# Block entries with three transposed sums, pooling data in the projection operands' memory, and an earlier begin in the last product

## The chip, the cores and the metric

The kernel runs on one core of one Trainium2 chip, in one launch. Time is device time in microseconds (us), from the start of the program to its end. A core has five engines with queues of their own, which work in parallel and meet through semaphores: TensorE (PE: matmuls and transposes; PEld is its weight load), VectorE (DVE), ScalarE (ACT), GpSimd (POOL) and SyncE (SP), which here only issues DMA transfers. Data lives in DRAM, in SBUF (128 partitions of on-chip memory) and in PSUM (eight banks of 128 x 512 floats, where TensorE writes its results and from which DVE and ACT read).

## The reference

The input is a sequence of 1024 tokens with 1024 channels, in float32. One layer is computed:

```python
h = x + 0.5 * swiglu(rms(x))                    # FFN1: w1, w3 1024 x 2816, w2 2816 x 1024
u = rms(h)
q, k, v, p, gates = split(u @ w_in)             # 3 x 768, 512 and 2 x 1024 columns
yA = dilated_mixture_attention(q, k, v) @ W_A   # 12 heads of 64, 3 groups of dilation 1, 4, 16
yB = multiscale_pool(p) @ W_B                   # 4 groups of 128 channels, windows 2, 4, 8, 16
h = h + (sigmoid(gA) * yA + sigmoid(gB) * yB) @ W_o
h = h + 0.5 * swiglu(rms(h))                    # FFN2
return rms(h)
swiglu(x) = (silu(x @ w1) * (x @ w3)) @ w2
```

`multiscale_pool` takes, for each of its four groups, trailing means over the tokens less the token itself, and applies a 128 x 128 map.

## The kernel before

**Stages.** By the trace, FFN1's up projections run until about 449 us and its down products from there to 670, the projections of the mix stage (`w_in`) from 670 to 1047, attention with the pooling branch and W_o from 1054 to 1302, FFN2 from there to the end. The 1024 tokens are eight tiles of 128 rows; `h[t]` holds tile t.

**Seven products.** Each large matrix product is done by 2 x 2 blocks with seven block products instead of eight. The right-hand blocks of the transposed activations are b11, b12 (tokens 512 to 1023, low channels), b21 (tokens 0 to 511, high channels) and b22. The products use seven sums of them, stored by name in the dictionary X (`SUMS`): b11, b21, b22 and

```python
t1 = b12 - b11;  t2 = b22 - t1;  t4 = t2 - b21;  t3 = b22 - b12
```

Products 1 and 2 use b11 and b21, made from tiles 0 to 3. The products 6, 7, 5, 4 and 3 (in this order) use t2, t3, t1, t4 and b22, which need tiles 4 to 7 as well. `Quad` (L319) does the seven products of one weight block: `operand(m)` makes the weight's sum, `run(m)` multiplies.

**Two parts of each number.** Every operand is held as a rounded part (hi) and a remainder (lo) in TensorE's fast format, and a product is hi·hi + hi·lo + lo·hi: 12 matmuls of 128 x 512 (L314) for one block product. `Sevens.split` makes both parts of a weight: ACT copies the hi part (L303), then POOL or DVE subtracts for the lo part (L306). `Rows` (L372) makes both parts of a token block: four transposes on TensorE into one PSUM bank (L381), ACT's copy of the bank (L382, `x_t`/`x_b` to `xhi`), and, in a later call, DVE's subtraction from the bank (`lower`, L385, `xlo`). PSUM banks come in two sets of four, tagged "mm" and "acc", which are handed out in the order of the program.

**Entries.** There are three places where the sums of a new activation are made: before FFN1's up projections, before the mix projections, before FFN2's up projections (`Entry`, L387; in the rows `f1`, `mix` and `f2`). At first the tiles 0 to 3 are transposed for b11 and b21 (`rows`, `rows_first`, `rows_first2`), beside the last steps of the stage ahead. Then `Entry.run` (L405) walks over the tiles 4 to 7: for each it runs two products i and k that need only b11 or b21 (m of 1 or 2), and between them transposes the tile's five blocks for b22, t1, t2, t4 and t3, 20 transposes in all. t1, t2 and t4 are computed by DVE in SBUF (L423 to L425), t3 by POOL (L426). `high(t, 0)` computes a tile's inverse root mean square (L263 on DVE, L264 on POOL), `high(t, 1)` scales the tile by it and by the gain (L267, 128 x 1024 on DVE); t1 and t3 overwrite the tile of b11 and b21. `operand(i + 2)` and `operand(k + 2)` make the weights of the next two products, `out(i)` takes a product's bank away, `more(n)` makes the weights of the first sum products.

**The order of work.** In all these stages the order of instructions on every engine's queue is that of the program text (`manual_schedule`). An instruction whose data is not there holds everything behind it on its engine.

**Down products.** `Down.run` (L720s) does the product with w2 in seven products m of several steps each. `begin(i)` makes a step's operands: the weights' sum on DVE (L684), hi parts on ACT and lo parts on DVE or, for every fourth, POOL (`bhi`, `blo`, `ahi`, `alo`; L664, L668). `multiply` runs a step's matmuls (L706), `add` adds a finished bank to `h` on DVE (L711), `load(i)` fetches what is needed three steps later. Step i's text is: multiply i, add (of the product before), load i+3, begin i+2. `tick` is a hook used by the first down product alone, where scaling and `rows_first` are hung in.

**End of the mix stage.** The mix loop runs `items` products; jobs near its end load what attention needs: `first_ring` twelve products before the end, values and the first branch weights (`load_values`, `load_branch`, on SP's queue) at the fourth from the end. The pooled groups are stored to DRAM from the mix stage (`pool_dram`, hi and lo). The sums of the mix activations lie in two pools, `xa` (b21, b11) and `xb`, both closed together at the end of the loop.

**Attention.** Its first statements load the four pooled groups, 1 MB each, into four tiles of their own (`load_pool`, L1605, groups 2, 3, 0, 1 in this order), then the queries and keys of the second head group (`load_ring`) and the second branch weights. For each of the 24 block pairs the loop runs scores (L1482), exponents on ACT, transposes, products with the values, and four or eight matmuls of the pooling branch (`branch`, L1619, output `yp`; 12 per product, which reads the four groups in the order 2, 3, 0, 1) as a filler. A finished `yp` is multiplied and stored (`end_branches`, `send`).

Of the kernel before, what the change touches and what calls it, by code (L numbers as in the profile page):

```python
# [16 lines left out]
P = 128  # L17
# [109 lines left out]
def tile_block(  # L127
# [244 lines left out]
    class Rows:  # L372


        def __init__(self, X, what, src, t, tag="acc"):
            q = t % 4
            self.hi, self.lo = (v[:, :, q * P:(q + 1) * P] for v in X[what])
            p = bank(tag, f"x_{what}_{t}")
# [5 lines left out]
        def lower(self):  # L384
            ve.tensor_tensor(self.lo, self.p, self.hi.bitcast(F32), op=OP.subtract)  # L385

    class Entry:  # L387
# [18 lines left out]
        def run(self, high, after, first=0):  # L406
# [3 lines left out]
            y = high(4, 1)  # L410
            for t in range(4, NT):
                i = first + 2 * (t - 4)
                k = i + 1
                self.product(i)
                if t + 1 < NT:
                    high(t + 1, 0)
                lo = self.low[t - 4]
                b11, b21, b12, b22 = lo[:, LOWS], lo[:, HIGHS], y[:, LOWS], y[:, HIGHS]
# [4 lines left out]
                ve.tensor_tensor(t1, b12, b11, op=OP.subtract)  # L423
                ve.tensor_tensor(t2, b22, t1, op=OP.subtract)
# [6 lines left out]
                self.operand(k + 2)  # L431
                rs = [Rows(X, what, src, t) for what, src in (("t1", t1), ("t2", t2), ("t4", t4), ("t3", t3))]
                if t + 1 < NT:
# [191 lines left out]
    class Down:  # L625
# [87 lines left out]
        def run(self, pool, after, tick=None):  # L713
# [6 lines left out]
            for i, (m, s) in enumerate(self.steps):  # L720
# [10 lines left out]
                ahead = i == n - 3 and tick is None  # L731
# [63 lines left out]
    def begin_up1():  # L795
# [23 lines left out]
        def rows(t, what, c):  # L819
            scaled_part(t, c, gain_row)  # L820
            r[t] = Rows(X, what, h[t][:, c], t)
# [27 lines left out]
        rows(3, "b11", LOWS)  # L849
# [5 lines left out]
        entry.operand(1)  # L855

# [16 lines left out]
        r[3].lower()  # L873
        entry.product(3)
# [23 lines left out]
    mstack, dstack = ExitStack(), ExitStack()  # L898
# [5 lines left out]
    def room1():  # L904
        scope.close()
        X_mix.update(sums_of_x(mstack.enter_context(sbuf("xa")), "mix", ("b21", "b11")))
        return down_room("f1")
# [271 lines left out]
    pool_in = {}  # L1179
# [24 lines left out]
    with sbuf("steps1", "right") as pool:  # L1204
# [90 lines left out]
    with tc.manual_schedule():  # L1295
# [4 lines left out]
        for k in range(len(items) + 4):  # L1300
# [27 lines left out]
            if k == len(items) - 12:  # L1328
                later.append([k, first_ring()])
# [823 lines left out]
```

## Time and profile before

| | |
|---|---|
| median of three runs | 1955.8 us (1953.81, 1955.8, 1956.05) |
| the profiled execution | 1956.69 us, its span 1954.5 us |
| mean granted TensorE clock | 0.994 |
| DMA | 333.57 MB, mean 171 GB/s |
| span of FFN1's start and entry, 0 to 66 us | PE busy 61.4 us, DVE 50.8 us |
| FFN1 behind its entry, 66 to 669.7 us | PE busy 602.2 us, DVE 403.5 us |
| mix stage, 669.7 to 1047 us | PE busy 372.1 us, DVE 264.2 us |
| attention to W_o, 1054 to 1302 us | PE busy 235.8 us, DVE 183.0 us, clock 0.96 |
| FFN2, 1302 to the end | PE busy 639.0 us, DVE 439.2 us |

A row of the profile names a line of the kernel (L314 is line 314), an engine, an operation, output and inputs by the program's names (buffer numbers left out), partitions x elements, and how many there are. In the timeline a row begins with its start and its duration, both in us; brackets give the idle time of the engine just before it and what ended it. Times are counted from the span's start. The profiled execution takes 2.2 us more than its span, since a run also holds what lies ahead of the first and behind the last instruction.

### The profile page before, as it was taken

The page shows a single profiled execution, that of the slowest core. Times are in us where ns is not written, and L with a number is a line of the kernel's source. Part 1 is how long each engine was busy: PE and PEld are TensorE (multiplying, and loading weights), DVE is VectorE, ACT ScalarE, POOL GpSimd, SP SyncE. Part 2 cuts the span into 40 slices and gives each one's busy share as a digit, 9 for nine tenths or more (in the row PEclk, how much of TensorE's full clock was granted, in tenths as well). Part 3 has the DMA queues.
Part 4 walks back from the last instruction along what each step waited for, and adds up shares of the span by engine and source line. Part 5 has one row for each costly group of instructions (what it writes and reads, how often), then busy time and mean ns, then how long its engine had stood idle before and what let it go on. Part 6 is the DMA issues. An engine that isn't in the chain of part 4 may idle for free. (4 is left out here: it accounts for less than half of the span.)

```text
span 1954.5 us, 25035 instructions
## 1 busy us (share of the span) xinstructions
PE 1917.3 (98%) x8938; PEld 1580.5 (81%) x8938; DVE 1344.2 (69%) x2020; ACT 762.8 (39%) x1371; POOL 738.1 (38%) x555
## 2 busy tenths in 40 slices
PE   9999999999999999999998999999999999999998
PEld 7788888887888887888876878887788888878886
DVE  7776556557676876658774887787666556577777
ACT  6333333334344533335344663253333333333344
POOL 4433333332223444445454365644333333322131
PEclk9999999999999999999998999999999999999999
DMA  4154223336476437665668887642523222454564
GB/s 185 44 194 164 90 86 113 125 119 214 151 239 213 167 116 235 224 224 183 222 234 281 222 254 253 253 184 78 203 97 128 100 86 103 156 187 138 198 205 162
DMA packets 147437, 333.57 MB, mean 171 GB/s; under 512 B 20208, under 2 KB 40944, under 8 KB 145776
## 3 DMA queue, kind: packets, MB, share of 16 engines
q1 hardware_dynamic: 138096, 307.22, 46.5%
q10 hardware_dynamic: 9216, 24.75, 3.6%
q8 instruction: 71, 1.16, 0.2%
q14 instruction: 54, 0.44, 0.1%
HBM read 229.61 MB, written 102.30 MB: 170 GB/s over the span
## 5 line engine op out<-in xcount | busy, mean ns | idle before, releaser
L706 PE MATMUL d_f<-bhi_f,alo_f 128*128 128x512 f32 x616 | 240.9, 391 | 3.9 <-POOL alo_f L668 3.5
L706 PE MATMUL d_f<-bhi_f,ahi_f 128*128 128x512 f32 x616 | 240.6, 391 | 0.0
L706 PE MATMUL d_f<-blo_f,ahi_f 128*128 128x512 f32 x616 | 239.7, 389 | 0.0
L668 POOL TENSOR_TENSOR alo_f<-g_f,ahi_f 128x512 fp32r<-128x512 f32 x68 | 96.7, 1440 | 287.9 <-ACT ahi_f L664 287.9
L314 PE MATMUL u_mixm<-xhi_t_mix,wc_mixm 128*128 128x512 f32 x608 | 195.8, 392 | 3.3 <-POOL wc_mixm L306 2.4
L314 PE MATMUL u_mixm<-xhi_b_mix,wc_mixm 128*128 128x512 f32 x456 | 149.4, 393 | 1.7 <-DVE y_m L985 1.5
L706 PEld LDWEIGHTS d_f<-bhi_f,alo_f 128*128 128x128 f32 x616 | 115.6, 188 | 31.8 <-POOL alo_f L668 6.5
L314 PEld LDWEIGHTS u_mixm<-xhi_t_mix,wc_mixm 128*128 128x128 f32 x608 | 113.6, 188 | 29.9 <-POOL wc_mixm L306 5.4
L706 PEld LDWEIGHTS d_f<-bhi_f,ahi_f 128*128 128x128 f32 x616 | 115.6, 188 | 24.1 <-ACT ahi_f L664 0.4
L706 PEld LDWEIGHTS d_f<-blo_f,ahi_f 128*128 128x128 f32 x616 | 115.7, 188 | 23.8
L314 PE MATMUL u_mixm<-xlo_t_mix,wc_mixm 128*128 128x512 f32 x304 | 118.5, 390 | 0.0
L306 POOL TENSOR_TENSOR wc_mixm<-s_mixm,wc_mixm 128x512 fp32r<-128x512 f32 x52 | 75.3, 1449 | 99.5 <-ACT wc_mixm L303 77.5
L314 PEld LDWEIGHTS u_mixm<-xhi_b_mix,wc_mixm 128*128 128x128 f32 x456 | 85.5, 188 | 20.7 <-ACT late_hi L1128 1.9
L303 ACT ACTIVATE wc_mixm<-s_mixm 128x512 fp32r<-128x512 f32 x76 | 47.6, 629 | 126.4 <-DVE s_mixm L347 47.9
L314 PE MATMUL u_mixm<-xlo_b_mix,wc_mixm 128*128 128x512 f32 x228 | 88.8, 389 | 0.0
L664 ACT ACTIVATE ahi_f<-g_f 128x1024 fp32r<-128x1024 f32 x84 | 81.8, 974 | 2.7 <-DMA g_f<-gs_f 2.7
L306 POOL TENSOR_TENSOR wc_mixm<-raw,wc_mixm 128x512 fp32r<-128x512 f32 x40 | 59.9, 1502 | 52.6 <-ACT wc_mixm L303 47.6
L664 ACT ACTIVATE bhi_f<-s_f2w 128x512 fp32r<-128x512 f32 x55 | 32.6, 627 | 95.3 <-DVE s_f2w L684 87.6
L1857 PE MATMUL wo<-w_o,o_hi 128*128 128x512 f32 x224 | 69.3, 390 | 0.0
L664 ACT ACTIVATE bhi_f<-s_f1w 128x512 fp32r<-128x512 f32 x55 | 33.0, 630 | 87.0 <-DVE s_f1w L684 82.3
L314 PEld LDWEIGHTS u_mixm<-xlo_t_mix,wc_mixm 128*128 128x128 f32 x304 | 57.1, 188 | 11.9 <-DVE xlo_t_mix L385 0.2
L1619 PE MATMUL yp<-pool_in,wab 128*128 128x512 f32 x192 | 56.4, 431 | 4.8 <-DMA pool_in<-pool 4.8
(1304 smaller groups left out, 5107.1 us busy)
## 6 DMA issues: line engine op xcount, KB each, us to landing
g_f<-gs_f SPq DMA_DIRECT2D x70, 512.0 KB, 4.6
gs_f<-y_f SPq DMA_DIRECT2D x88, 256.0 KB, 2.3
raw<-in_w2a_dram SPq DMA_DIRECT2D x35, 512.0 KB, 4.1
raw<-in_w2b_dram SPq DMA_DIRECT2D x35, 512.0 KB, 4.1
gs_f<-gb_f SPq DMA_DIRECT2D x46, 256.0 KB, 2.3
raw<-in_w1a_dram SPq DMA_DIRECT2D x22, 512.0 KB, 4.6
raw<-in_w3a_dram SPq DMA_DIRECT2D x22, 512.0 KB, 6.3
raw<-in_w1b_dram SPq DMA_DIRECT2D x22, 512.0 KB, 4.6
```

Of the source, the lines that this page charges most:

```text
L303: ac.activation(w[:, 0], src, AF.Copy)
L306: eng.tensor_tensor(w[:, 1], src, w[:, 0].bitcast(F32), op=OP.subtract)
L314: pe.matmul(p, a, b, start=(start and k == 0 and q == 0), stop=(k == 3 and q == 2), skip_group_check=not start)
L664: ac.activation(hi[:, c], src, AF.Copy)
L668: eng.tensor_tensor(lo[:, d], src[:, o], hi[:, d].bitcast(F32), op=OP.subtract)
L706: pe.matmul(self.banks[m][t], l, r, start=(first and q == 0), stop=(last and q == 2))
L1619: pe.matmul(p, a, b, start=(j == 0), stop=(j == 11))
L1857: pe.matmul(banks[m][t], l, r, start=(st == 0 and j == 0 and q == 0), stop=(st == 1 and j == 1 and q == 2))
```

## The change

1. **Entries.** Per tile 4 to 7 only b22, b12 and t3 are transposed: 12 transposes instead of 20. The other sums are built in PSUM by DVE: b12's transposed bank less the kept transposed b11 gives t1, in place; t3's bank plus b11 gives t2, in another bank; t2 less the kept transposed b21 gives t4, in place. The new class `Parts` makes both parts from such a bank, without transposes. The next tile's scaling and its t3 come one tile earlier in the text (`scaled_rows`), and `operand(k + 2)` comes later, behind `fourth()`. The last tile has an order of its own.
2. **Kept blocks.** So that the transposed b11 and b21 are at hand, `Rows.keep` copies the transposed bank back over the half of `h[t]` from which it was made: 8 copies of 128 x 512 on ACT for each of the three entries.
3. **Last product.** In the second down product, in all steps of its last m, `begin(i + 2)` is placed before the adds and the load; before, at one step alone.
4. **Pooling loads.** The four tiles of their own are gone. Groups 2 and 3 are loaded into the two parts of the mix activations' b11 at the fifth product from the end of the mix loop, groups 0 and 1 into b21 at the third from the end, behind the values and the first branch weights. `xa` stays open to the end of attention.

```diff
@@ class Rows
-            p = bank(tag, f"x_{what}_{t}")
+            p = self.flat = bank(tag, f"x_{what}_{t}")
+        def keep(self, dst):
+            ac.activation(dst.rearrange("p (k q) -> p k q", k=4), self.p, AF.Copy)
+
+    class Parts:
+        def __init__(self, X, what, src, t):
+            q = t % 4
+            self.hi, self.lo = (v[:, :, q * P:(q + 1) * P] for v in X[what])
+            self.src = src.rearrange("p (k q) -> p k q", k=4)
+            ac.activation(self.hi, self.src, AF.Copy)
+        def lower(self):
+            ve.tensor_tensor(self.lo, self.src, self.hi.bitcast(F32), op=OP.subtract)
@@ Entry.run
-            y = high(4, 1)
+            def scaled_rows(t):
+                y = high(t, 1)
+                t3 = self.sv.half_tile("s", f"t3_{t}")
+                gp.tensor_tensor(t3, y[:, HIGHS], y[:, LOWS], op=OP.subtract)
+                return y, t3
+            y, t3 = scaled_rows(4)
             for t in range(4, NT):
...
+                last = t == NT - 1
+                b11, b21 = (self.low[t - 4][:, c] for c in (LOWS, HIGHS))
+                def second():
+                    ve.tensor_tensor(t2, r3.flat, b11, op=OP.add)
+                    return Parts(X, "t2", t2, t)
+                def fourth():
+                    ve.tensor_tensor(t2, t2, b21, op=OP.subtract)
+                    return Parts(X, "t4", t2, t)
                 self.product(i)
...
-                s = Rows(X, "b22", b22, t)
-                t1, t3 = b11, b21
-                t2, t4 = (self.sv.half_tile("s", f"{n}_{t}") for n in ("t2", "t4"))
-                ve.tensor_tensor(t1, b12, b11, op=OP.subtract)
-                ve.tensor_tensor(t2, b22, t1, op=OP.subtract)
-                ve.tensor_tensor(t4, t2, b21, op=OP.subtract)
-                gp.tensor_tensor(t3, b22, b12, op=OP.subtract)
-                s.lower()
+                s = Rows(X, "b22", y[:, HIGHS], t)
+                p12 = bank("acc", f"x_b12_{t}")
+                for j in range(4):
+                    c = slice(j * P, (j + 1) * P)
+                    pe.transpose(p12[:, c], y[:, c], ident)
+                r3 = Rows(X, "t3", t3, t)
+                t2 = bank("acc", f"x_t2_{t}")
+                if last:
+                    r2 = second()
+                ve.tensor_tensor(p12, p12, b11, op=OP.subtract)
+                r1 = Parts(X, "t1", p12, t)
+                if not last:
+                    s.lower()
                 self.operand(i + 2)
                 self.out(i)
                 self.product(k)
-                self.operand(k + 2)
-                rs = [Rows(X, what, src, t) for what, src in (("t1", t1), ("t2", t2), ("t4", t4), ("t3", t3))]
-                if t + 1 < NT:
-                    y = high(t + 1, 1)
-                for r in rs:
-                    r.lower()
+                if last:
+                    r2.lower()
+                    r3.lower()
+                    r1.lower()
+                    self.more(1)
+                    r4 = fourth()
+                    s.lower()
+                    r4.lower()
+                else:
+                    y, t3 = scaled_rows(t + 1)
+                    r2 = second()
+                    r1.lower()
+                    r3.lower()
+                    r2.lower()
+                    r4 = fourth()
+                    self.operand(k + 2)
+                    r4.lower()
                 self.out(k)
                 after(t)
-                if t >= NT - 2:
-                    self.more(t - NT + 2)
+                if t == NT - 2:
+                    self.more(0)
@@ Down.run
-                ahead = i == n - 3 and tick is None
+                ahead = tick is None and m == len(DOWN) - 1 and i + 2 < n
@@ FFN1, tiles 0 to 3
-        rows(3, "b11", LOWS)
+        rows(3, "b11", LOWS, "mm")
...
         entry.product(0)
         entry.operand(1)
+        for t in range(4):
+            r[t].keep(h[t][:, LOWS])
...
         squares(5, square2)
         r[3].lower()
+        for t in range(4):
+            r[t].keep(h[t][:, HIGHS])
@@ pooling loads
+    def load_pool(g, x, part):
+        y_pool[g] = X_mix[x][part].rearrange("p (q k) c -> p q (k c)", q=2)
+        nc.sync.dma_start(y_pool[g].bitcast(F32), pool_dram[g])
@@ rows_first of the mix entry, lower(t, rs) of FFN2's
+            for r, c in zip(rs, (LOWS, HIGHS)):
+                r.keep(h[t][:, c])
@@ mix loop
+            if k == len(items) - 5:
+                load_pool(2, "b11", 0)
+                load_pool(3, "b11", 1)
             if k == len(items) - 4:
                 load_values(0, row_part)
                 load_branch(0)
+            if k == len(items) - 3:
+                load_pool(0, "b21", 0)
+                load_pool(1, "b21", 1)
@@ attention
-        for g in (2, 3, 0, 1):
-            load_pool(g)
         load_ring(uses[1], ring_tile)
```

More of the change, by code (lines that the diff above doesn't have):

```diff
@@ L905, in room1 @@
         scope.close()
-        X_mix.update(sums_of_x(mstack.enter_context(sbuf("xa")), "mix", ("b21", "b11")))
+        X_mix.update(sums_of_x(xstack.enter_context(sbuf("xa")), "mix", ("b21", "b11")))
         return down_room("f1")
@@ L1339, in tile_block @@
     left_b = ExitStack()
-    y_pool = [left_b.enter_context(sbuf(f"pool{g}")).tile([P, 2, S], F32R, name=f"pool_in{g}") for g in range(4)]
     sums_o = left_b.enter_context(sbuf("sums_o"))
@@ L1788, in tile_block @@
     left_b.close()
+    xstack.close()
     x2, m1 = ExitStack(), ExitStack()
@@ L1881, in scaled2, with lower @@
         scaled(t, h[t] if t < 4 else rows_y[t], gain2)
-    def lower(rs):
+    def lower(t, rs):
         for r in rs:
             r.lower()
+        for r, c in zip(rs, (LOWS, HIGHS)):
+            r.keep(h[t][:, c])
     with tc.manual_schedule():
```

22 lines of the change are left out of this document (9 added, 13 removed).

## The prediction

> **What bounds the kernel now.** I read the page's busy times first, then TensorE's waits and busy time by stage, then the timeline of the stages that the change touches.
>
> ```profile
> PE 1917.3 (98%) x8938; PEld 1580.5 (81%) x8938; DVE 1344.2 (69%) x2020; ACT 762.8 (39%) x1371; POOL 738.1 (38%) x555
> ```
> ```profile
> 30.00:66.00 36.00, 34.70 (x189) 28.15 (x188) 30.92 (x42) 20.57 (x39) 21.74 (x16) 1.00 0.14 45
> 660.00:704.00 44.00, 43.07 (x228) 35.67 (x227) 34.93 (x50) 24.46 (x46) 25.07 (x19) 1.00 0.19 71
> ...
> 1283.00:1338.00 55.00, 52.51 (x274) 43.08 (x274) 46.15 (x70) 28.11 (x51) 24.94 (x18) 1.00 0.28 100
> ```
> ```profile
> 1050.00:1075.00 25.00, 18.53 (x86) 12.73 (x84) 6.77 (x25) 7.87 (x22) 4.09 (x4) 0.74 1.01 373
> ```
> In a window row the first number is its length, then each engine's busy time, the granted TensorE clock, DMA share and GB/s. TensorE (PE) is busy 98% of the span, so only two things help: fewer matmul slots, or the 37 us in which it is idle or slowed. The three entries (first three rows) hold 1.3, 0.9 and 2.5 us of idle time; the start of attention alone holds 6.5 us, at a mean clock of 0.74. DVE is busy for 31 of 36 us in the first entry: it is the next engine there.
>
> **Part 1, pooling data loaded earlier.** Before, the four loads (L1605, 1 MB each) follow everything else on SP's queue.
>
> ```profile
> PE yp L1619 <- DMA pool_in<-pool: 4.8, 2, 3.5
> ```
> ```profile
> DMA to landing us min/median/max: 9.3/14.0/18.2
> ```
> ```profile
> 1041.24 0.39 PE L314 MATMUL u_mixm<-xhi_b_mix,wc_mixm 128*128 128x512 f32 x1
> ...
> 1054.19 4.40 SPq L1605 DMA_DIRECT2D pool_in<-pool  x4
> ...
> 1064.26 1.63 PE L1619 MATMUL yp<-pool_in,wab 128*128 128x512 f32 x3
> ...
> 1072.33 1.22 PE L1619 MATMUL yp<-pool_in,wab 128*128 128x512 f32 x2 [3.48 <-DMA pool_in<-pool]
> 1073.48 0.58 PE L1482 MATMUL s<-qk_hi,qk_hi 64*128 64x256 f32 x2
> ...
> 1078.21 1.15 ACT L1155 ACTIVATE qk_hi<-qk_in 128x512 fp32r<-128x512 f32 x2 [0.55 <-DMA qk_in<-rot]
> ...
> 1085.52 0.40 PE L1482 MATMUL s<-qk_in,qk_hi 64*128 64x128 f32 x2
> ```
> ```profile
> 1041.40:1047.00 5.60, 5.60 (x27) 4.63 (x26) 1.20 (x2) 5.06 (x10) 5.11 (x5) 1.00 0.24 94
> 1059.00:1077.00 18.00, 11.69 (x53) 7.86 (x53) 5.46 (x28) 7.20 (x21) 0.00 (x0) 0.58 0.99 362
> 1061.80:1065.20 3.40, 2.63 (x8) 1.80 (x9) 0.53 (x3) 2.88 (x12) 0.00 (x0) 0.50 0.99 399
> ...
> 1078.80:1082.20 3.40, 3.40 (x30) 2.93 (x30) 1.90 (x6) 2.53 (x10) 2.55 (x2) 0.99 0.97 333
> ```
> The first pooling product starts at 1064.26; its seventh and eighth matmul, on the third load, wait until 1072.33, and the next scores start at 1073.48. The DMA engines are full all that time (0.99 from 1059 to 1077).
>
> In the changed kernel loads 2 and 3 go into b11's two halves. b11's last reader, the product of the last projection's first sum, ends at about 1041.5 (first timeline row), SP has nothing to issue there before the late weights' store, and from 1041.4 to 1047 the DMA engines are 0.24 busy. 2.1 MB at the 0.42 MB per us of the full stretches is 5.0 us: it fits. Loads 0 and 1 go into b21 behind the values and the first branch weights, so they take the places in the queue that 2 and 3 had: issue at 1054.19, first landing 9.3 us later at 1063.5, before the product starts. Nothing is queued behind a new wait on SP except stores whose data come later anyway.
>
> So the eight matmuls run on: 8 x 0.43 us (half clock, 1.63 us for three overlapping) from 1064.26 is 1067.7, and the scores start 5.8 us earlier. What is late next is the second head group's queries and keys, queued behind the pooling loads: ACT waits for them at 1078.21. They move by the 2.1 MB that left the full stretch, 5.0 us, to 1073.2, and through ACT, the exponents and the key half the scores of that group move from 1085.5 to 1079.5 or 1080.5. I take **5.5 us**; bounds 3 (another queue entry, such as the next branch weights, is the limit) and 8 (the clock returns earlier as well).
>
> The clock is 0.50 in the third row and full again by the fourth; it fell when TensorE had been idle for about 1.3 us waiting for the first exponents, before any pooling wait, so I leave the first fall in and let the second half of the slow stretch go only as far as the loads allow. The Trainium skill, "TensorE: Matmul & The Clock Gate" (Part 1), has the clock halved only after an idle window of about 3.4 us and full after one busy window. The trace disagrees with its first half (an idle stretch much shorter came before the fall). By that rule the changed kernel would keep the full clock there; see the fourth rival.
>
> **Part 2, the entries.** Per tile 4 to 7, five blocks were transposed (20 transposes); now three (12), the other sums being built by DVE in PSUM.
>
> ```profile
> 669.75:677.47 7.72, 7.72 (x45) 6.59 (x44) 6.16 (x9) 5.70 (x11) 4.79 (x4) 1.00 0.11 45
> ```
> ```profile
> 672.96 0.60 PE L381 MATMUL x_t<-ident,h 128*128 128x128 f32 x4
> ...
> 674.62 0.47 PE L314 MATMUL u_mixm<-xhi_b_mix,wc_mixm 128*128 128x512 f32 x1
> ...
> 698.33 0.47 PE L314 MATMUL u_mixm<-xhi_t_mix,wc_mixm 128*128 128x512 f32 x1
> ...
> 702.67 0.73 PE L314 MATMUL u_mixm<-xhi_t_mix,wc_mixm 128*128 128x512 f32 x2 [0.61 <-POOL wc_mixm L306]
> ```
> ```profile
> 676.68 0.68 DVE L423 TENSOR_TENSOR h<-hn_mix,h 128x512 f32<-128x512 f32 x1
> 677.40 0.69 DVE L424 TENSOR_TENSOR s_mixt<-hn_mix,h 128x512 f32<-128x512 f32 x1
> ...
> 679.35 1.93 DVE L267 SCALAR_TENSOR_TENSOR hn_mix<-h,nst,gain_mix 128x1024 f32<-128x1024 f32 x1
> 681.95 2.48 DVE L385 TENSOR_TENSOR xlo_t_mix<-x_t,xhi_t_mix 128x512 fp32r<-128x512 f32 x4 [0.67 <-ACT xhi_t_mix L382]
> ...
> 710.30 0.93 DVE L306 TENSOR_TENSOR wc_mixm<-s_mixm,wc_mixm 128x512 fp32r<-128x512 f32 x1 [0.78 <-ACT wc_mixm L303]
> ```
> ```profile
> 680.15 3.51 POOL L306 TENSOR_TENSOR wc_mixm<-raw,wc_mixm 128x512 fp32r<-128x512 f32 x2
> ...
> 705.69 1.29 POOL L306 TENSOR_TENSOR wc_mixm<-s_mixm,wc_mixm 128x512 fp32r<-128x512 f32 x1 [1.37 <-ACT wc_mixm L303]
> ```
> Removed: 16 transposes took 674.62 - 672.96 = 1.66 us, so one is 0.104 us, 8 are 0.83 us a tile, 3.3 us an entry, 10.0 us in all, if TensorE stays the limit. A tile took 7.72 us with TensorE always busy, and would take 6.89.
>
> But DVE's work per tile does not shrink, and it now has a chain. In order: t1 0.72 (a result used by the next, 676.68 to 677.40), b22's lower half 0.62 (2.48 / 4), the next tile's scaling 1.93, t2 0.62, three lower halves 1.86, t4 0.62, then a wait for ACT's copy of t4, 0.78 (as before L306 at 710.30), its lower half 0.62, the inverse 0.06: 7.8 us from one t1 to the next. No row shows DVE writing a bank; its rows reading one (0.62) and those with both inputs in SBUF beside a busy POOL (1.7) bound it, and I take 0.62 as nearest. Bounds for the tile: 7.2 (scaling at 1.28, as in the clear) and 9.0 (two waits, scaling 2.34).
>
> Behind that chain stands the weight of the next tile's second product (the operand call moved behind t4): t4 ends 6.4 us after t1 starts, ACT's copies of t4 and of the weight take 0.6 each and POOL 1.29 to 1.75, so it is ready at 9.0. Counted from tile 4's first transpose: t1 0.85, tile 5's transposes 6.89 (second product 9.85, late by 1.7), tile 6's 15.35, tile 7's 23.15, last product until 28.2; t2's lower half is ready at 27.4, so the first sum product starts at 28.2 and the next, waiting for its weight as before, at 31.3. Before: 698.33 and 702.4, from 669.75, are 28.6 and 32.6. **Gain 1.3 us**, not 3.3.
>
> ```profile
> 26.03 1.68 POOL L306 TENSOR_TENSOR wc_f10a<-raw,wc_f10a 128x512 fp32r<-128x512 f32 x1 [1.82 <-PE u_f11a L314]
> ...
> 31.30 0.60 PE L381 MATMUL x_b<-ident,x 128*128 128x128 f32 x4
> ...
> 65.10 0.74 PE L314 MATMUL u_f10a<-xhi_t_f,wc_f10a 128*128 128x512 f32 x2 [0.62 <-POOL wc_f10a L306]
> ```
> ```profile
> 681.32 2.07 ACT L382 ACTIVATE xhi_t_mix<-x_t 128x512 fp32r<-128x512 f32 x4 [1.09 <-PE x_t L381]
> ```
> ```profile
> 1302.37 0.60 PE L381 MATMUL x_b<-ident,hn_f 128*128 128x128 f32 x4
> ...
> 1336.37 0.73 PE L314 MATMUL u_f20a<-xhi_t_f,wc_f20a 128*128 128x512 f32 x2 [0.62 <-POOL wc_f20a L306]
> ```
> FFN1's entry has in addition a multiply of 0.6 us on DVE in two tiles, which makes 32.4 to the same point, against 33.5 before (65.10 less 0.3, from 31.30): 1.1 us. But eight copies on ACT are added (0.52 us each by the four in 2.07). The first four fill a pause; the second four stand before ACT's copy of the first m=2 weight, which POOL finishes at 27.7 for a product that starts at 28.5 (2.75 us before 31.30). 2.0 us later there is 1.2 us of stall, 1.0 with POOL in the clear. **Gain 0** (bounds -2.5 and +4). FFN2: 31.9 against 33.7, less 0.5 for copies that hold banks a little longer in front of the transposes of rows 2 and 3: **1.3** (-1.5 to +5). In the mix stage the copies lie beside the down steps and cost nothing; if that cover were gone, 8 x 0.52 = 4.2 us. The memory place of rows 3 in FFN1 (another bank) costs nothing: it only keeps the copies from being waited for.
>
> **Part 3, the last product.**
>
> ```profile
> PE d_f L706 <- POOL alo_f L668: 2.0, 3, 0.8
> ```
> ```profile
> 1934.05 0.50 PE L706 MATMUL d_f<-bhi_f,alo_f 128*128 128x512 f32 x1 [0.74 <-POOL alo_f L668]
> ```
> Operands of the last four steps are now begun before the adds. DVE works without a pause there, the same operations in another order, so the last operand is ready when it was; the 0.74 us at 1934.05 goes, and may come back at the last step. **0.5 us** (-0.5 to 2.0).
>
> **Sum.** 5.5 + 1.3 + 0 + 1.3 + 0.5 = 8.6 us. The profiled execution took 1956.7, so 1948.1; the median of the runs shown is 1955.8, 0.9 under it: **1947.2 us**. Its own range, from the middle of each bound, is 1943 to 1951.
>
> **Rivals.**
> A. TensorE stays the limit in the entries: the 10.0 us of transposes come off whole, and about 2 of the stalls. 5.5 + 12 + 0.5 = 18: 1937.8. For it: DVE was busy only 6.16 of 7.72 us in the first tile. Against: the sum of 7.8.
> B. The wait only moves: attention is held by the next transfers (3.0), the entries break even or lose a little (-1 together): 2 us, 1953.8, no change.
> C. Slower: the weight behind t4 sets the period of each entry tile. From a chain of over 8.3 us a tile loses more than its transposes gave; at the upper bound, 9.0 + 0.7 of POOL contention, 2.0 us over 7.72 in 12 tiles is 24 less the 6 gained elsewhere: 18 us, 1974; at 9.0 alone it is 15 - 6 = 9, 1965. For it: POOL's 3.51 for two, the fixed order of each queue. Against: operands in PSUM keep t1, t2 and t4 clear of POOL.
> D. The clock does not fall at the start of attention: the eight matmuls and the scores after them save 8 x 0.2 + 0.7 = 2.3 us if the keys are there: 1944.9. Against: the exponents' wait stays.
>
> **How the numbers follow.** Forecast 0.50, A 0.12, B 0.20, C 0.10, D 0.08. No change here means within 0.2%, 3.9 us, which is about what a measurement of this kernel can tell. The forecast, A, D and 0.06 of B's 0.20 (its upper bounds) are faster: 0.76; the rest of B is no change, 0.14; C is slower, 0.10. The range 1938 to 1957 holds the forecast, D, B and half of A, and leaves out C.
>
> **What would show it.** Right: the loads of pooling data in two pairs, no yp wait for them, next scores 5 to 6 us earlier after the mix stage; 96 transposes fewer; in the entries TensorE waiting for POOL's weight or a lower half about 1.7 us a tile, DVE without pauses. Wrong: entry tiles at 6.9 us without waits (A), at 9 or more (C), the second group's keys landing no earlier than 1078 (B), a clock of 1.00 at the first pooling product (D).

## The result, and the profile after

| | median (us) | ratio to the kernel before, 95% interval |
|---|---|---|
| before | 1954.29 | |
| changed kernel | 1952.69 | 0.9995 [0.9987, 1.0002] |

The change makes no difference that can be told from none: 1.6 us, where 8.6 were forecast. The profiled execution of the changed kernel took 1955.09 us, its span is 1953.3 us, 1.2 under that of before. Two large parts cancel. First the page's busy times, then the start times of a few tiles' matmuls in both kernels (count, shortest/median/longest in ns, first and last start):

```profile
PE 1910.2 (98%) x8842; PEld 1571.7 (80%) x8842; DVE 1337.3 (68%) x2020; ACT 776.9 (40%) x1395; POOL 725.2 (37%) x555
```
Before:
```profile
L314 PE MATMUL u_f11a<-xhi_t_f,wc_f11a x32: 388/389/389, 89.3 to 100.0; 128*128 128x512 f32 x32
L1619 PE MATMUL yp<-pool_in,wab x192: 387/395/796, 1064.3 to 1195.5; 128*128 128x512 f32 x192
L1857 PE MATMUL wo<-w_o,o_hi x224: 387/389/477, 1203.9 to 1299.2; 128*128 128x512 f32 x112
L314 PE MATMUL u_f28a<-xhi_t_f,wc_f28a x32: 389/389/389, 1620.9 to 1634.3; 128*128 128x512 f32 x32
```
After:
```profile
L314 PE MATMUL u_f11a<-xhi_t_f,wc_f11a x32: 388/389/389, 90.9 to 101.5; 128*128 128x512 f32 x32
L1678 PE MATMUL yp<-xhi_b_mix,wab x96: 387/397/775, 1068.2 to 1191.3; 128*128 128x512 f32 x96
L1915 PE MATMUL wo<-w_o,o_hi x224: 387/389/477, 1200.5 to 1296.4; 128*128 128x512 f32 x112
L314 PE MATMUL u_f28a<-xhi_t_f,wc_f28a x32: 389/389/389, 1619.9 to 1633.3; 128*128 128x512 f32 x32
```

The 96 transposes are gone (8938 - 8842). Read downwards, the changed kernel's lag is +1.6 us behind FFN1's entry (90.9 - 89.3), +3.9 at the first pooling product (1068.2 - 1064.3), -3.4 when W_o starts (1200.5 - 1203.9), -1.0 in FFN2 (1619.9 - 1620.9) and -1.2 at the end. So **attention won 7.3 us** (from +3.9 to -3.4), and what surrounds it gave back 6.1, nearly all of it in the three entries and the copies just ahead of them.

**Attention.** Windows of 3.4 us and the timeline of the changed kernel:

```profile
1063.20:1066.60 3.40, 2.05 (x18) 1.48 (x18) 2.44 (x16) 2.50 (x5) 0.00 (x0) 0.84 1.05 417
1066.60:1070.00 3.40, 3.38 (x10) 2.32 (x11) 1.12 (x2) 2.89 (x12) 0.00 (x0) 0.50 1.00 406
1070.00:1073.40 3.40, 3.40 (x21) 2.40 (x20) 0.66 (x3) 1.12 (x6) 0.00 (x0) 0.65 1.00 402
1073.40:1076.80 3.40, 3.40 (x24) 3.05 (x22) 2.69 (x9) 2.57 (x6) 0.77 (x1) 1.00 0.64 192
```
```profile
1068.17 1.63 PE L1678 MATMUL yp<-xhi_b_mix,wab 128*128 128x512 f32 x3
...
1071.86 0.58 PE L1544 MATMUL s<-qk_hi,qk_hi 64*128 64x256 f32 x2
...
1075.32 1.15 ACT L1206 ACTIVATE qk_hi<-qk_in 128x512 fp32r<-128x512 f32 x2 [0.54 <-DMA qk_in<-rot]
...
1081.67 0.40 PE L1544 MATMUL s<-qk_in,qk_hi 64*128 64x128 f32 x2
```

The eight pooling matmuls run on without a wait. Counted from the first of them, the next scores come 3.69 us later, against 9.22 before (1073.48 - 1064.26): 5.5 us won, where 5.8 were worked out. The second group's keys follow 7.15 us later against 13.95, 6.8 won where 5.0 were worked out, and that group's scores 13.5 against 21.3 (1085.52 - 1064.26), 7.8 won. The clock is full again in the fourth row; by the first three rows it stood at half for about 6.9 us (2 x 3.4 x (0.16 + 0.50 + 0.35)), against 17 before.

**Entries.** TensorE's waits in the changed kernel (sum, times, longest); then the timeline at the end of FFN1's entry, filtered to PE, DVE, ACT and POOL, and the window behind it:

```profile
PE u_f20a L314 <- DVE xlo_t_f L385: 3.2, 1, 3.2
PE u_f10a L314 <- DVE xlo_t_f L385: 3.2, 1, 3.2
PE u_mixm L314 <- DVE xlo_t_mix L385: 3.2, 1, 3.2
...
PE d_f L753 <- ACT ahi_f L711: 1.6, 1, 1.6
PE x_b L381 <- ACT h_again L389: 1.4, 1, 1.4
```
```profile
31.12 0.60 PE L381 MATMUL x_b<-ident,x 128*128 128x128 f32 x4
...
55.03 0.60 PE L381 MATMUL x_t<-ident,s_f1t 128*128 128x128 f32 x4
...
61.95 0.69 PE L314 MATMUL u_f10a<-xhi_t_f,wc_f10a 128*128 128x512 f32 x1 [3.19 <-DVE xlo_t_f L385]
```
```profile
54.91 1.78 DVE L345 TENSOR_TENSOR s_f10a<-raw 128x512 f32<-128x512 f32 x1
56.73 0.69 DVE L347 TENSOR_TENSOR s_f10a<-s_f10a,raw 128x512 f32<-128x512 f32 x1
59.15 0.70 DVE L441 TENSOR_TENSOR x_t<-x_t,x 128x512 f32<-128x512 f32 x1 [1.73 <-ACT xhi_t_f L382]
...
60.51 0.69 DVE L401 TENSOR_TENSOR xlo_t_f<-x_t,xhi_t_f 128x512 fp32r<-128x512 f32 x1
61.12 0.68 DVE L385 TENSOR_TENSOR xlo_t_f<-x_t,xhi_t_f 128x512 fp32r<-128x512 f32 x1
```
```profile
57.51 0.63 ACT L303 ACTIVATE wc_f10a<-s_f10a 128x512 fp32r<-128x512 f32 x1 [2.23 <-DVE s_f10a L347]
58.05 0.58 ACT L382 ACTIVATE xhi_b_f<-x_b 128x512 fp32r<-128x512 f32 x1
58.53 0.59 ACT L382 ACTIVATE xhi_t_f<-x_t 128x512 fp32r<-128x512 f32 x1
```
```profile
54.87 1.28 POOL L306 TENSOR_TENSOR wc_f12b<-raw,wc_f12b 128x512 fp32r<-128x512 f32 x1 [1.95 <-ACT wc_f12b L303]
```
```profile
61.00:64.40 3.40, 2.45 (x6) 2.00 (x7) 3.33 (x7) 1.88 (x5) 0.60 (x1) 0.65 0.00 0
```

The lines are the changed kernel's: L441 makes t2, L460 t1, L445 t4, and L401 is the lower part of `Parts`. Tile 7's three blocks are transposed by 55.6 (last transposes at 55.03). Their copies on ACT (L382) start at 58.05, since ACT's queue has the weight of the first sum product in front (L303 at 57.51, from `more(0)`), and that waits for its sum on DVE (L345 and L347, until 57.4). L345 takes 1.78 us: it reads two tiles in SBUF, while POOL subtracts a weight (L306 at 54.87). t2 (L441) starts 0.03 us after ACT's copy of t3's bank has ended, in all three entries, though both only read that bank; whether the program's bookkeeping or the chip asks for this order was not settled. TensorE's next product needs t2's lower part (L401) and, as will be shown, the bank that t3's lower part (L385) gives back. It stands still for 3.19 us, and then the clock is down to a mean of 0.65 over 3.4 us.

From tile 4's first transpose to the first sum product it takes:

| us | FFN1 | mix | FFN2 |
|---|---|---|---|
| before | 28.87 | 28.58 | 29.07 |
| changed kernel | 30.83 | 30.72 | 31.03 |
| early k+2 alone | 29.01 | 28.74 | 29.94 |
| late weight | 29.02 | 28.90 | 30.66 |
| late weight, early k+2 | 27.24 | 26.96 | 29.58 |
| the same, weight on POOL | 27.25 | 26.98 | 28.13 |
| the same, i+2 and out(k) early | 26.92 | 26.95 | 27.58 |

The last five rows are experiments, told now.

### The profile page after: what moved, and what is told of

It is laid out like the page before. It is cut to its first block, busy times and chain, and to the rows that moved or that the text cites. A ratio compares the mean times of both kernels' runs of the same rounds, so it can differ in the third digit from the quotient of the medians.

```text
span 1953.3 us, 24868 instructions
## 1 busy us (share of the span) xinstructions
PE 1910.2 (98%) x8842; PEld 1571.7 (80%) x8842; DVE 1337.3 (68%) x2020; ACT 776.9 (40%) x1395; POOL 725.2 (37%) x555
## 5 line engine op out<-in xcount | busy, mean ns | idle before, releaser
L306 POOL TENSOR_TENSOR wc_mixm<-s_mixm,wc_mixm 128x512 fp32r<-128x512 f32 x52 | 74.8, 1439 | 101.6 <-ACT wc_mixm L303 84.3
L303 ACT ACTIVATE wc_mixm<-s_mixm 128x512 fp32r<-128x512 f32 x76 | 47.7, 629 | 126.3 <-DVE s_mixm L347 44.4
L306 POOL TENSOR_TENSOR wc_mixm<-raw,wc_mixm 128x512 fp32r<-128x512 f32 x40 | 57.6, 1442 | 66.2 <-ACT wc_mixm L303 62.2
L715 DVE TENSOR_TENSOR alo_f<-g_f,ahi_f 128x1024 fp32r<-128x1024 f32 (+1 forms) x44 | 52.7, 1197 | 7.1 <-ACT ahi_f L711 7.1
```

Source lines behind the costliest of these rows:

```text
L303: ac.activation(w[:, 0], src, AF.Copy)
L306: eng.tensor_tensor(w[:, 1], src, w[:, 0].bitcast(F32), op=OP.subtract)
L715: eng.tensor_tensor(lo[:, d], src[:, o], hi[:, d].bitcast(F32), op=OP.subtract)
```

## The experiments

Times are medians; the kernel before was measured beside each group, at 1953.9, 1953.1, 1952.8 and 1954.3 us. Differences between runs of different groups carry this spread of 1.5 us.

**1. The pooling loads alone, and all but them.** The first is the kernel before with part 4 of the change; the second the changed kernel with the loads back at the start of attention.

```diff
 # first: the kernel before
+            if k == len(items) - 5:
+                load_pool(2, "b11", 0)
+                load_pool(3, "b11", 1)
...
-        for g in (2, 3, 0, 1):
-            load_pool(g)
 # second: the changed kernel, the same lines the other way
```

> The kernel before with the pooling loads alone (part 4 of the change). Theory: the traces of before and after lag by +3.9 us when the first pooling product starts and by -3.4 us when W_o starts, so the loads are worth 7.3 us wherever the rest stands: 7 us under before (5.5 to 8.5). Rival: part of those 7.3 us is only the entries' lag taken up by a wait that was there anyway; then 3 to 4 us under before.

> The changed kernel with the pooling loads where they were. Theory: what is left is the three entries' loss, 1.6 + 2.1 + 1.7 us, less 0.3 at the last product: 5 us over before (3.5 to 6.5), with a wait of about 3.2 us of TensorE before the first sum product in each entry and the half clock behind it. Rival (the loss of the entries is absorbed by the wait for the pooling loads): within 1.5 us of before.

Measured: the loads alone 1947.27 us, ratio 0.9963 [0.995, 0.9977], 6.6 us under before; all but the loads 1957.17, ratio 1.0015 [1.0007, 1.0024], 3.3 us over. The first is as the theory had it; the second shows the loss of the entries by itself, just under the theory's span and far from the rival's absorption. The two parts are separate and of opposite sign. Their sum, 3.3 under before, is 1.7 us more than the 1.6 of the whole change; that rest was not followed up.

**2. The weight of the first sum product later.** `more(0)` is taken from the end of tile 6 and put behind tile 7's transposes, in one kernel ahead of t2, in the other behind t1.

```diff
-                if t == NT - 2:
-                    self.more(0)
...
                 if last:
+                    self.more(0)          # "late weight"
                     r2 = second()
                 ve.tensor_tensor(p12, p12, b11, op=OP.subtract)
                 r1 = Parts(X, "t1", p12, t)
+                if last:
+                    self.more(0)          # the other kernel: here instead
```

> The changed kernel with the weight of the first sum product (more(0)) moved behind the three transposed blocks of tile 7, ahead of t2. Order on DVE is unchanged; on ACT the copies of b22 and t3 now stand ahead of the weight's copy. Theory (ACT's queue): t2 no longer waits for a copy held behind the weight; in FFN1 and mix it starts at the end of the weight's second sum, 1.7 us earlier, the wait of 3.2 us falls to 0.6 to 1.5 and the half clock behind it goes; in FFN2 the lower part of that weight is on DVE ahead of t2 and little is won (0.3): 5 to 9 us under the changed kernel. Rival (DVE's sums are late by themselves, 1.8 us beside POOL, and ACT's order is no matter): within 1 us of the changed kernel.

> As before, but the weight is moved behind t2 and t1 on DVE too. Theory: in FFN1 and mix t2's lower part is ready when TensorE is, the weight's lower part 1.5 to 2.1 us later, so a wait of 1 to 2 us stands at the first sum product's third matmul, and FFN2 wins the same now: 5 to 11 us under the changed kernel, more than the other placement if FFN2 decides. Rival (the weight is the late operand in any order): 0 to 2 us under the changed kernel, waits of 3 us at the weight instead of the lower part.

Measured: ahead of t2 1945.73 us, ratio 0.9953 [0.9941, 0.9966], 7.0 under the changed kernel; behind t1 1947.6, ratio 0.9969 [0.9958, 0.998], 5.1 under. The first kernel's timeline in FFN1's last tile, on ACT, DVE and PE, and the windows behind the first sum product in FFN1, mix and FFN2:

```profile
55.86 0.61 ACT L382 ACTIVATE xhi_t_f<-x_t 128x512 fp32r<-128x512 f32 x1
57.73 0.63 ACT L303 ACTIVATE wc_f10a<-s_f10a 128x512 fp32r<-128x512 f32 x1 [1.27 <-DVE s_f10a L347]
```
```profile
55.13 1.78 DVE L345 TENSOR_TENSOR s_f10a<-raw 128x512 f32<-128x512 f32 x1
...
57.56 0.69 DVE L441 TENSOR_TENSOR x_t<-x_t,x 128x512 f32<-128x512 f32 x1
```
```profile
60.35 0.47 PE L314 MATMUL u_f10a<-xhi_t_f,wc_f10a 128*128 128x512 f32 x1 [1.37 <-DVE xlo_t_f L385]
```
```profile
60.00:63.60 3.60, 3.25 (x14) 2.60 (x15) 3.52 (x6) 2.10 (x4) 1.29 (x1) 1.00 0.00 0
697.00:700.60 3.60, 2.85 (x13) 2.40 (x14) 3.52 (x7) 2.07 (x5) 1.11 (x2) 1.00 0.00 0
1322.40:1326.00 3.60, 3.01 (x8) 2.41 (x9) 3.04 (x6) 2.08 (x5) 1.16 (x1) 0.53 0.01 2
```

The copy of t3 runs 2.7 us earlier, t2 follows the sums at once, TensorE's wait is 1.37 us instead of 3.19 in FFN1 and in mix, and the clock stays at 1.00 behind it. In FFN2, where the weight's lower part stood on DVE ahead of t2, the wait is still 2.8 us and the clock falls to 0.53. The theory holds in all three entries; the rival (ACT's order is no matter) falls. The other placement is not better: its first sum product still waits 1.5 us in FFN1 and mix (by the profile for one of ACT's copies, not for a lower part) and 2.9 in FFN2, so the advantage expected there did not come.

**3. operand(k+2) early, the weight on POOL, and two more places.**

```diff
 # on top of "late weight"
                 else:
+                    self.operand(k + 2)
                     y, t3 = scaled_rows(t + 1)
...
                     r4 = fourth()
-                    self.operand(k + 2)
                     r4.lower()
 # on top of that
-                     lambda n: first.A.operand((6, 7)[n]))
+                     lambda n: first.A.operand((6, 7)[n], (gp, None)[n]))
 # on top of that
                 r3 = Rows(X, "t3", t3, t)
+                self.operand(i + 2)
...
                     r4 = fourth()
+                    self.out(k)
                     r4.lower()
```

> The late weight (more(0) behind tile 7's transposes), and operand(k+2) back in front of the next tile's scaling, as before the change, so that it no longer stands behind t4. Theory (POOL beside DVE): that weight's lower part then runs about 2 us earlier, the first sum of the first sum product (1.78 us beside POOL) takes 0.7 instead, t2 follows 1.1 us earlier, TensorE's wait before the first sum product falls from 1.4 to about 0.3 in FFN1 and mix and from 2.8 to 1.7 in FFN2, whose half clock goes: 3 to 6 us under the late weight alone (1945.7). Rival (the early weight collides with the scaling instead, 1.9 for 1.3, and the tiles get longer): 0 to 3 us over it.

> The same, with the lower part of the first sum product's weight on POOL in FFN1 and FFN2 (only FFN2 changes, there it was on DVE). Theory: DVE is freed of 0.7 us and of a wait of 0.8 ahead of t2, FFN2's wait falls by 1.4: 1 to 2 us under the one with operand(k+2) early. Rival (POOL is later than DVE with it): no change, with a wait for POOL's weight at the third matmul.

> The same as the last, and in each tile operand(i+2) ahead of t1 and out(k) between t4 and its lower part. Theory (ACT's order delays the weight by the copy of t1, DVE waits 0.67 us for ACT's copy of t4): the waits of 0.4 to 0.7 for POOL's weight go, and the tiles come down to 7.2 to 7.5 us: 2 to 5 us under the last. Rival (TensorE is already the limit of the tiles by then): within 1 us of it.

Measured: 1940.64 us, ratio 0.9937 [0.9925, 0.995], 5.1 under the late weight; 1937.39, ratio 0.992 [0.9907, 0.9934], 3.2 under that; 1936.75, ratio 0.9915 [0.9902, 0.9929], 0.6 under that. The first step gave the time that was expected, and FFN2's half clock went, though the waits only fell to 0.70 us in FFN1 and mix and 2.1 in FFN2 (0.3 and 1.7 expected). In the second, FFN2's wait fell from 2.1 to 0.7 us as expected; the rest of its 3.2 us is not in the entries: the two profiled executions, 6.4 us apart, differ by 4 us before FFN2's entry already, with waits for exponents of 3.8 and 1.6 us in attention. The edit does not touch attention, so I take this for spread from one execution to another; that was not shown. The third missed: the tiles were at 7.25 to 7.55 us in FFN1 already, and came to 7.27 to 7.36 only.

**4. operand(k+2) early, alone.** The same move in the changed kernel, with `more(0)` left at the end of tile 6.

> The changed kernel with operand(k+2) back in front of the next tile's scaling, and nothing else. Theory: the first sum of tile 7 runs in 0.7 us beside an idle POOL instead of 1.78, so everything behind it on DVE and ACT comes 1.1 us earlier; the wait falls from 3.2 to 2.1 us in each entry, and at 2.1 the clock stays: 3 us an entry, 6 to 10 us under the changed kernel (1952.7). Rival (only ACT's order counts; POOL's work goes on elsewhere): within 1 us of it.

Measured: 1946.98 us, ratio 0.9964 [0.9951, 0.9976], 5.7 under the changed kernel, a little short of the expected 6. Its timeline on POOL, DVE and PE in FFN1, and the window behind the first sum product:

```profile
51.01 1.29 POOL L306 TENSOR_TENSOR wc_f12b<-raw,wc_f12b 128x512 fp32r<-128x512 f32 x1
```
```profile
54.30 0.68 DVE L345 TENSOR_TENSOR s_f10a<-raw 128x512 f32<-128x512 f32 x1
...
57.43 0.70 DVE L441 TENSOR_TENSOR x_t<-x_t,x 128x512 f32<-128x512 f32 x1 [1.73 <-ACT xhi_t_f L382]
```
```profile
60.23 0.51 PE L314 MATMUL u_f10a<-xhi_t_f,wc_f10a 128*128 128x512 f32 x1 [2.49 <-DVE xlo_t_f L385]
```
```profile
60.00:63.60 3.60, 3.37 (x9) 2.68 (x10) 3.52 (x6) 2.15 (x4) 1.28 (x1) 0.57 0.00 0
```

POOL's subtraction is done before DVE's sum, which takes 0.68 us instead of 1.78, and t2 starts 1.72 us earlier (57.43 against 59.15). But it still waits 1.73 us for ACT's copy of t3, behind the weight. The wait fell to 2.49 us only, since TensorE too came earlier, and the clock still fell (0.57). That part of the expectation was wrong.

**5. The standing time filled.** 24, then 11 matmuls of 128 x 128 without a use behind the last product of each entry, in the changed kernel.

```diff
                 if last:
+                    idle = bank("mm", f"idle_{self.sv.name}")
+                    for _ in range(24):       # 11 in the second
+                        pe.matmul(idle[:, :P], ones, ones, start=True, stop=True)
                     r2.lower()
```

> The changed kernel with 24 matmuls of 128 x 128 without a use put in the wait before the first sum product of each entry (about 2.6 of the 3.2 us). The wait for t2's lower part stays where it is. Theory (the clock falls because TensorE stands still for some 3 us): the clock stays at 1.00 in the rows behind the wait, and each entry ends 1.7 to 2.0 us earlier: 5 to 6 us under the changed kernel (1952.7). Rival (the slow first matmuls have another cause, such as the operands just written): within 1 us of the changed kernel.

> The changed kernel with 11 matmuls of 128 x 128 without a use in the wait before the first sum product, in place of 24: each of the 24 ran as two passes of 0.115 us, and they overran the wait by 2.1 us. 11 are 2.5 us of the 3.2. Theory (the clock falls because TensorE stands still): the clock stays at 1.00 behind the wait, the first sum product starts where it did, and each entry ends 1.7 to 2.0 us earlier: 5 us under the changed kernel (1952.7; 3 to 7). Rival (the clock falls for the data wait, not for the standing): within 1 us of the changed kernel, matmuls 0.43 us apart behind the wait.

Measured: with 24, 1957.31 us, ratio 1.0021 [1.0012, 1.0029], 4.6 over the changed kernel; with 11, 1950.08, ratio 0.9984 [0.9975, 0.9993], 2.6 under. Each matmul ran as two passes, so 24 filled 5.5 us, and the first sum product came 1.9 us late in each entry (in FFN1 32.77 us behind tile 4's first transpose, against 30.83). That is 0.3 us an entry more than the half clock it saves, 1.0 in all; the rest of the 4.6 is open. With 11 they fit. Below: their row, the product behind them and the window; then the first sum product's rows in the changed kernel and in this one.

```profile
59.37 2.62 PE L470 MATMUL idle_f<-ones 128*128 128x128 f32 x22
62.71 0.47 PE L314 MATMUL u_f10a<-xhi_t_f,wc_f10a 128*128 128x512 f32 x1 [0.73 <-DVE xlo_t_f L385]
```
```profile
61.20:64.60 3.40, 2.67 (x15) 2.20 (x15) 3.33 (x7) 1.87 (x5) 0.04 (x1) 1.00 0.00 0
```
```profile
L314 PE MATMUL u_f10a<-xhi_t_f,wc_f10a x32: 389/389/687, 61.9 to 74.3; 128*128 128x512 f32 x32
```
```profile
L314 PE MATMUL u_f10a<-xhi_t_f,wc_f10a x32: 388/389/468, 62.7 to 73.5; 128*128 128x512 f32 x32
```

The wait for data ends where it did (30.85 us behind tile 4's first transpose, against 30.83), but the clock is 1.00 in the windows behind it in all three entries, and this block's products take 10.8 us (62.7 to 73.5) instead of 12.4 (61.9 to 74.3): the half clock costs 1.6 us an entry where it comes. It falls because TensorE stands still: behind the unfilled stands of 2.5 to 3.2 us it fell in ten of eleven places in the profiles of this case, behind the filled ones in none of six. The gain of 2.6 us is just under the expected 3 to 7; three times 1.6 would be 4.8. Part of the rest is lost at once: the next weight block's first sum product (`u_f10b`, `u_f20b`) comes 1.2 us earlier in FFN1 and 1.5 in FFN2 (44.90 and 44.82 us behind tile 4's first transpose, against 46.13 and 46.33). And the falls do not come in every execution. In the changed kernel without the loads, the same program up to the end of FFN1, the profile has the same wait of 3.18 us in FFN1, but the clock stays at 1.00 behind it and the block takes 10.8 us:

```profile
L314 PE MATMUL u_f10a<-xhi_t_f,wc_f10a x32: 388/389/467, 62.3 to 73.1; 128*128 128x512 f32 x32
```

Over the executions of the changed kernel the mean clock ran from 0.992 to 0.997, and the profiled one had 0.993. How often the falls come in the others was not measured.

**6. The last product's order alone,** in the fastest kernel.

```diff
-                ahead = tick is None and m == len(DOWN) - 1 and i + 2 < n
+                ahead = i == n - 3 and tick is None
```

> The fastest version so far (late weight, early operand(k+2), weight on POOL, operand(i+2) early, out(k) early; 1936.75) with the last product's begin order of the kernel before. It measures part 3 alone. Theory (the waits of 2.0 us between the steps go, a wait of 1.4 for the last step's left operand and a half clock come in their place): 0 to 1.5 us over it. Rival (they go for good): 2 us over it.

Measured: 1937.96 us, ratio 0.9918 [0.9904, 0.9931], 1.2 over, as the theory had it; the intervals overlap, so the size is uncertain. In the last 40 to 20 us of the span TensorE is busy 10.00 of 10.00 us in both windows of 10 us of the changed kernel, against 8.70 and 9.26 before; the wait of 1.6 us for the last left operand (`ahi_f` in the waits above) is new. In the changed kernel's profile the clock falls behind this wait too: it is 0.61 from 1940.1 to 1943.5 us, with matmuls 0.43 us apart, and of the change of order only 0.2 us is left (the lead is 1.0 us in FFN2 and 1.2 at the end). It stays at 1.00 there in the profiles of the kernel before and of the fastest kernel.

**7. Which lower part releases the first sum product.** On top of the fastest kernel:

```diff
                     r2 = second()
+                    r3.lower()
+                    r2.lower()
                 ve.tensor_tensor(p12, p12, b11, op=OP.subtract)
...
                 if last:
-                    r2.lower()
-                    r3.lower()
                     r1.lower()
```

> The fastest version so far (1936.75, where TensorE still stands 0.7 us before the first sum product of each entry) with t3's lower part, and behind it t2's, directly behind t2 in tile 7, ahead of t1. Theory (the bank): the first sum product takes over the bank of t3's transposed block, and what releases it in the rows is t3's lower part (L385), 0.15 us before it starts, not t2's (L401), which is ready 0.6 us earlier. With both one place earlier the wait of 0.7 goes in each entry: 1.5 to 2.1 us under. Rival (t2's own lower part, or the weight's on POOL, is what it waits for): the wait stays at 0.5 to 0.7, within 0.6 us of it.

Measured: 1939.08 us, ratio 0.9928 [0.9914, 0.9942], 2.3 over the fastest kernel. TensorE's timeline in FFN1, in the fastest kernel and in this one:

```profile
58.17 0.47 PE L314 MATMUL u_f10a<-xhi_t_f,wc_f10a 128*128 128x512 f32 x1 [0.70 <-DVE xlo_t_f L385]
```
```profile
57.28 0.39 PE L314 MATMUL u_f10a<-xhi_t_f,wc_f10a 128*128 128x512 f32 x1
...
60.73 0.50 PE L314 MATMUL u_f10a<-xhi_t_f,wc_f10a 128*128 128x512 f32 x1 [0.51 <-ACT wc_f10a L303]
...
62.15 0.73 PE L314 MATMUL u_f10a<-xhi_t_f,wc_f10a 128*128 128x512 f32 x2 [0.69 <-POOL wc_f10a L306]
```

The wait of 0.70 us before the first sum product is gone in all three entries. Both lower parts had been moved, so the run alone does not tell them apart, but the rows do: the product starts at 57.28, while t2's lower part (L401) runs until 57.39, and in the changed kernel that part was ready at 61.20, 0.75 us before the product started. So it was t3's lower part, and as the product does not read t3, the bank. But t1 now comes 1.3 us later on DVE and the next weight's sum 0.7, and the second sum product waits 0.51 + 0.69 us for that weight instead: by the next weight block the entry is 0.8 us longer in FFN1 and 0.7 in FFN2 than in the fastest kernel. The mechanism was right, and more than the gain went into the next wait.

## Why the prediction was right in its wide range and wrong in its sum

- **Pooling loads: mechanism right, size low.** 5.5 us were forecast, 7.3 (in the profiles) and 6.6 (alone) measured, inside the bounds of 3 to 8. What was too small is the second group's keys (5.0 worked out, 6.8 measured) and the earlier return of the clock, which only the upper bound named; how the rest splits between them was not shown. The fourth rival (the clock does not fall) did not come: the first fall, at the wait for exponents, stayed (0.84 and 0.50 in the first two windows).
- **The tiles of the entries: right.** In mix, tiles 5, 6 and 7 were to start 6.89, 15.35 and 23.15 us behind tile 4; they started 7.16, 15.35 and 22.89 behind (at 678.76, 686.95 and 694.49, from 671.60). TensorE waited for POOL's weight in them, as forecast, but by 0.2 to 0.7 us where it stands in the rows, not 1.7; and POOL's neighbourhood made DVE no slower where it reads a bank. So the slower rival, a weight that sets the period, did not come, nor did TensorE as the limit.
- **The end of the entries: wrong, and this is the step that failed.** "t2's lower half is ready at 27.4, so the first sum product starts at 28.2": it started at 30.7 in mix and 30.8 and 31.0 in the others. The chain was carried on from tile to tile as if tile 7 were like the rest. Ahead of tile 7 the queues also hold `more(0)`: two sums on DVE, one of them at 1.78 us beside POOL, and a copy on ACT that waits for them, with tile 7's own copies behind it. Before the change t2 was made in SBUF, so no sum of tile 7 had to wait for those copies. Experiments 2 and 4 take the two causes away one by one, and both together (the first kernel of experiment 3) bring the entry to 27.0 in mix. So forecast gains of 0, 1.3 and 1.3 us in FFN1, mix and FFN2 became losses of 1.6, 2.0 and 1.8, by the lag behind each entry less the lag ahead of it. The order on ACT could be read in the trace of before: there, too, the first sum product's weight stands ahead of tile 7's first copy, while its sum on DVE (L345 at 692.07) still took 0.68 us.

```profile
693.58 0.63 ACT L303 ACTIVATE wc_mixm<-s_mixm 128x512 fp32r<-128x512 f32 x1 [1.98 <-DVE s_mixm L347]
694.12 0.58 ACT L382 ACTIVATE xhi_b_mix<-x_b 128x512 fp32r<-128x512 f32 x1
```

The half clock behind that wait, 1.6 us, was in no step of the prediction either; it is paid by waits that the next product no longer has (from the first sum product to the product in the first rows above it is 28.95 us in FFN1, against 29.13 before).

- **The kept copies: nearly right.** In FFN1 the forecast stall of 1.0 us came as 0.3: in the product of that weight the third matmul starts at 28.71, 0.52 us behind the second, where 0.23 is the rule. Tile 4's transposes come at 31.12 against 31.30 all the same, since the first product began 0.7 us earlier; in FFN2 TensorE waits 1.4 us for a copy where it had waited 0.8 for a lower part, 0.6 more, where 0.5 was put; in mix 0.5 us where nothing was put.
- **Last product: right in kind, its size uncertain.** 0.5 was forecast, with the remark that the wait may come back at the last step, which it did: 1.6 us in place of 0.74. Measured are 1.2 with overlapping intervals in the fastest kernel, and 0.2 in the profiles of before and after, where a half clock followed that wait; the prediction had no such fall.
- The sum of 8.6 us was wrong because the entries' term had the wrong sign: +2.6 forecast, -5.4 measured, and 0.9 more lost ahead of the entries of mix and FFN2, where the waits for copies stand. The time lies outside the forecast's own range (1943 to 1951) and near the second rival's 1953.8. That nearness is chance: there attention was to win 3.0 and the entries to lose 1, where 7.3 and 6.3 were measured. Only the wide range of 1938 to 1957 holds the time, and 0.76 had been put on a faster kernel, 0.14 on the outcome that came. The first rival's time, 1937.8, is about what the reordered kernel reached (1936.75), but not by its mechanism: its tiles still wait for POOL's weight.

For the slow sum beside POOL, the Trainium skill ("GPSIMD Engine Reference", section 1, Specifications) says that POOL shares its way into SBUF with DVE, and that the two collide when DVE reads two operands from SBUF. The rows agree: the sum of two SBUF tiles takes 0.68 us alone and 1.78 beside POOL, while operations with one operand in a bank stay at 0.68 to 0.70 (as L441 and the lower parts from 34.66 to 37.13 us, beside POOL's work from 34.31 to 37.14).

## What to carry to other kernels

When the path is walked for a loop, walk its last round separately, with everything that stands in each queue for what follows the loop: here the work for the next stage held the copies on which the last round depended. An instruction that waits costs what is queued behind it, so a sum and the copy that waits for it belong behind the copies that are ready. And a stall that is only moved to another operand wins nothing: take it away, then look what is late next.

## What the runs showed of the hardware

In the entries the clock of TensorE fell behind single stands of 3.2 us (three entries of the changed kernel, but only two of the one without the loads), 2.9, 2.8 and 2.5 us, and did not behind 2.1, 1.5, 1.4 and 0.7 us. The Trainium skill ("TensorE: Matmul & The Clock Gate", Part 1) puts the fall behind an idle window of about 3.4 us; here 2.5 us of standing was enough in all three entries of experiment 4, and 2.5 us of useless matmuls in place of most of the stand kept it away. But the length of one stand is not the whole rule. At the start of attention the clock fell within a window with TensorE busy 2.05 of 3.40 us (the first window row above), whose one long stand is 1.35 us. And in the last product the same stand of 1.58 to 1.59 us had a half clock behind it in four profiled executions (the changed kernel 0.61, early k+2 alone 0.73, the weight behind t1 0.70, 11 fillers 0.64, each in a window of 3.4 us) and none in two (late weight with early k+2, weight on DVE or on POOL: 1.00). What decides was not measured.
